# Keeping B's operands in DRAM, splitting two of seven products again, and weighing A's rows on ScalarE, in a 4096-cubed matmul with GELU

## The chip, the cores and the metric

The kernel runs on one core of a Trainium2 chip. Its time is the device time of the execution in microseconds (us). Before the change it took 1579.29 us (median of three runs). The traces are of single executions, so their spans differ by a few us from the medians.

Words used throughout: TensorE multiplies (PE in the profile; PEld is its weight load), VectorE (DVE) adds, subtracts and transposes, ScalarE (ACT) copies out of PSUM and applies functions, GpSimd (POOL) and SyncE (SP) issue DMAs. VectorE and ScalarE do their instructions in program order; the case in group 4 below shows VectorE idle for 8.13 us with a sum waiting behind a late transposition.

## The reference

```python
m, k, n = 4096, 4096, 4096            # a, b: random normal, float32
x = np.matmul(a, b)
return 0.5 * x * (1 + np.tanh(np.sqrt(2 / np.pi) * (x + 0.044715 * x**3)))
```

## The kernel before

It multiplies in fp16 by Strassen's scheme at the level of the whole matrices: each of A, B and the result has four quadrants, and seven products M1 to M7 replace eight. The result is made in 16 groups: a row block of A (four of them, 512 rows in each half) by a column block of B (four, 512 columns in each half). A group is 7 products of 64 matmuls, done in 4 steps each. A step is 16 matmuls of 128x512. Operand sums are made by VectorE two steps ahead, in three rotating buffers:

```python
PRODUCTS = [
    ("M3", "Y", "11", ("12", "22", 1)),          # name, chain, operand of A, operand of B
    ("M5", "X", ("11", "12", -1), "22"),
    ("M7", "X", ("12", "22", -1), ("21", "22", 1)),
    ...                                            # M1, M4, M2, M6
]
# in make_sums: one 128x2048 sum for one step
    t = pool.tile([P, 4 * NC], F16, name=tag, tag=tag, bufs=AHEAD + 1)
    nc.vector.tensor_tensor(out=x, in0=y, in1=z, op=ALU.add if o[2] > 0 else ALU.subtract)
```

A block of A comes in eight chunks of 1 MB in fp16 (quadrant and half of its depth), cast from float32 by four DMAs of 256 KB from GpSimd into one of two staging buffers, then turned by VectorE with one transposition of 2.3 us. The next block is loaded while the last group of the old one and the first group of the new one run (group gi and gi+1; `at(group, product, step, ...)`):

```python
            if na:                                 # the next group has another block of A
                at(gi, 4, c, load, (load_a, (mb1, "11", c)))
                at(gi, 5, 2 * c, turn_a, mb1, "11", c)
                at(gi, 5, 2 * c + 1, load, (load_a, (mb1, "12", c)))
                at(gi, 6, 2 * c, turn_a, mb1, "12", c)
                ...                                # "22" and "21" in the same manner
```

A step takes 3.45 us. B is read anew, cast by DMA, in nearly every group. A guard sums squares of A and B over rows and columns and falls back to a plain bf16 multiplication if magnitudes vary too much; ScalarE squares and VectorE adds, on the blocks in the form in which they are multiplied (A's turned). A's blocks change between groups 3 and 4, 7 and 8, 11 and 12.

## Time and profile before

| | before |
|---|---|
| median time | 1579.29 us |
| TensorE busy | 1567.7 us, 99% |
| VectorE, ScalarE busy | 1233.7 us (78%), 518.0 us (33%) |
| TensorE's waits | 4.2 us in four places |
| HBM traffic | 285 MB read, 67 MB written |
| a 256 KB piece of A, issue to landing (median) | 6.8 us |

The prediction below shows the lines behind the first rows and reads them. Two more lines are in the view of DMA issues (tile written and read, queue, operation, count, size, median us from issue to landing):

```profile
stage<-in_a_dram POOLq DMA_DIRECT2D x112, 256.0 KB, 6.8
```

and in the list of all waits (waiting engine, tile and line; what ended the wait; us in total, times, longest):

```profile
DVE aT L161 <- DMA stage<-in_a_dram: 39.9, 14, 10.8
```

VectorE's transposition waits for A's pieces now and then, most of it at the start, but TensorE never notices.

### The profile page before, as it was taken

How to read it: one execution, taken by the hardware profiler on the slowest of the kernel's cores; microseconds unless marked ns; L12 is line 12 of the kernel's file. 1: busy time of each engine (PE TensorE's matmuls, PEld its weight loads, DVE VectorE, ACT ScalarE, POOL GpSimd, SP SyncE). 2: the span in 40 equal slices, each digit the busy share in tenths (PEclk: the TensorE clock that was granted, in tenths of full speed). 3: DMA queues.
4: the chain of work that ended last, by engine and by line, in shares of the span. 5: the costliest groups of instructions: out<-in, count | busy, mean ns of one | idle time of the engine just before them, and what ended most of it. 6: DMA issues, size and time to landing. Idle time of an engine off the chain costs nothing. (4 is left out here: it accounts for less than half of the span.)

```text
span 1577.1 us, 19678 instructions
## 1 busy us (share of the span) xinstructions
PE 1567.7 (99%) x7246; PEld 709.6 (45%) x7246; DVE 1233.7 (78%) x1381; ACT 518.0 (33%) x710; POOL 537.7 (34%) x980
## 2 busy tenths in 40 slices
PE   9999999999999999999999999999999999999998
PEld 4444444444444444444444444444444444444443
DVE  1698888967787888895778778887687778988775
ACT  1036445311122545531111344542211145364111
POOL 7753442420234144341124413245011443314400
PEclk9999999999999999999999999999999999999999
DMA  9999884882968378686597937679468885747802
GB/s 173 198 215 189 132 162 79 161 162 48 193 106 158 87 131 160 108 179 115 87 161 117 186 72 142 146 113 182 79 121 146 134 160 93 151 105 134 161 28 82
DMA packets 225047, 211.13 MB, mean 134 GB/s; under 512 B 20144, under 2 KB 192176, under 8 KB 224944
## 3 DMA queue, kind: packets, MB, share of 16 engines
q0 software_dynamic: 187648, 142.67, 61.7%
q1 hardware_dynamic: 37296, 67.13, 11.8%
q8 instruction: 59, 0.97, 0.2%
q14 instruction: 44, 0.36, 0.1%
HBM read 285.22 MB, written 67.11 MB: 223 GB/s over the span
## 5 line engine op out<-in xcount | busy, mean ns | idle before, releaser
L331 PEld LDWEIGHTS <-aS 128*128 128x128 f16 x4960 | 485.3, 98 | 587.2 <-issue 2.2
L186 POOL DMA_DIRECT2D bR<-in_b_dram x832 | 447.6, 544 | 700.0 <-DVE bS L302 329.7
L302 DVE TENSOR_TENSOR aS<-aT 128x2048 f16<-128x2048 f16 (+1 forms) x312 | 376.1, 1212 | 151.0 <-PE accX L331 114.5
L331 PE MATMUL accX<-bS,aS 128*128 128x512 f16 x1984 | 431.1, 379 | 0.0
L302 DVE TENSOR_TENSOR bS<-bR 128x2048 f16<-128x2048 f16 x310 | 376.1, 1218 | 69.3 <-PE accX L331 58.5
L331 PEld LDWEIGHTS <-aT 128*128 128x128 f16 x1984 | 194.2, 98 | 234.8 <-issue 0.8
L422 ACT ACTIVATE y<-y 128x512 f32<-128x512 f32 x192 | 118.5, 630 | 351.8 <-DVE y L431 351.4
L331 PE MATMUL accY<-bS,aS 128*128 128x512 f16 x992 | 216.7, 379 | 1.8 <-DVE y L431 1.8
L331 PE MATMUL accY<-bS,aT 128*128 128x512 f16 x992 | 216.9, 379 | 0.5 <-DVE bS L302 0.5
L331 PE MATMUL accX<-bS,aT 128*128 128x512 f16 x992 | 216.7, 379 | 0.0
L331 PE MATMUL accX<-bR,aS 128*128 128x512 f16 x992 | 216.7, 379 | 0.0
L331 PE MATMUL accY<-bR,aS 128*128 128x512 f16 x992 | 216.7, 379 | 0.0
L186 POOL DMA_DIRECT2D stage<-in_a_dram x144 | 89.9, 630 | 249.0 <-DVE aT L161 178.0
L431 DVE TENSOR_TENSOR energy<-energy,square 128x1024 bf16<-128x1024 bf16 x240 | 164.4, 685 | 9.5 <-ACT square L207 5.7
L395 ACT COPY x<-accX 128x512 f32<-128x512 f32 x128 | 74.9, 585 | 224.3 <-PE accX L331 224.3
L207 ACT ACTIVATE square<-aT 128x1024 bf16<-128x1024 f16 x120 | 123.4, 1051 | 70.6 <-DVE energy L431 70.2
L207 ACT ACTIVATE square<-bR 128x1024 bf16<-128x1024 f16 x120 | 123.0, 1050 | 62.5 <-DVE energy L431 60.5
L161 DVE STREAM_TRANSPOSE aT<-stage 128x2048 uint32<-128x2048 uint32 (+1 forms) x37 | 74.6, 2017 | 46.0 <-DMA stage<-in_a_dram 39.9
L395 ACT COPY m<-accX 128x512 f32<-128x512 f32 x60 | 34.7, 579 | 215.7 <-PE accX L331 213.6
L422 ACT ACTIVATE y<-accX 128x512 f32<-128x512 f32 x64 | 38.2, 597 | 100.1 <-PE accX L331 99.9
L431 DVE TENSOR_TENSOR x<-accX,x 128x512 f32<-128x512 f32 x64 | 44.0, 691 | 21.8 <-ACT y L422 19.1
L431 DVE TENSOR_TENSOR y<-accY,m 128x512 f32<-128x512 f32 x60 | 39.9, 687 | 12.5 <-ACT m L395 12.4
(38 smaller groups left out, 344.9 us busy)
## 6 DMA issues: line engine op xcount, KB each, us to landing
bR<-in_b_dram POOLq DMA_DIRECT2D x832, 128.0 KB, 5.2
out_dram<-y SPq DMA_DIRECT2D x256, 256.0 KB, 5.7
stage<-in_a_dram POOLq DMA_DIRECT2D x112, 256.0 KB, 6.8
stage<-in_a_dram POOLq DMA_DIRECT2D x32, 128.0 KB, 5.1
row<-seen_d SPq DMA_DIRECT2D x2, 1.5 KB, 4.2
seen_d<-seen SPq DMA_DIRECT2D x1, 3.0 KB, 7.4
```

Source lines behind the costliest of these rows:

```text
L161: nc.vector.transpose(dst[:, :, x, :], src[:, :, x, :])
L186: nc.gpsimd.dma_start(out=dst, in_=src)
L207: nc.scalar.activation(t[:, :], src, ACT.Square)
L302: nc.vector.tensor_tensor(out=x, in0=y, in1=z, op=ALU.add if o[2] > 0 else ALU.subtract)
L331: nc.tensor.matmul(acc[:, :], sa[:, j // 2, i * P : (i + 1) * P, j % 2], sb[:, j, :], start=start and j == 0, stop=stop and j == 3, skip_g ...
L395: nc.scalar.copy(out=t[:, :], in_=src[:, :])
L422: nc.scalar.activation(y[:, :], src[:, :], ACT.Gelu_apprx_tanh)
L431: nc.vector.tensor_tensor(out=o[:, :], in0=x[:, :], in1=y[:, :], op=op)
```

## The change

Its intent is fewer matmul columns. In six groups M3 and M5 are each split by the same seven-product scheme again, one level down. That needs more and other sums, so to free VectorE the operands of B are made once, written to DRAM and fetched later; and the sums of squares of A leave VectorE for ScalarE, which squares each staged row with an accumulated output. The core of the diff (cuts marked):

```diff
+SPLIT_GROUPS = (8, 11, 12, 13, 14, 15)
+CHECK_GROUP = 9
+TURNS = ((2, 2), (3, 1), (5, 2), (6, 1), (7, 0), (7, 3), (8, 2), (9, 1))
+    def weigh_rows(mb, quad, c, xs):
+        s = staged[mb, quad, c]
+        ...
+            nc.scalar.activation(
+                weighed[mb, quad, c][:, :RUN], s[:, x, :], ACT.Square, accum_out=weighed[mb, ih][:, k, x : x + 1]
+            )
+            if tag == "bS" and gi == last_raw[nb]:
+                keep_operand((nb, name, q // 2), q % 2, t[:, :])      # SyncE writes it to DRAM
+    def multiply_split(gi, s, p):                                     # one of seven subproducts
+        for r in range(RT // 2):
+            ...
+            for j in range(NJ):
+                wide = p == "2" and j == 0
+                nc.tensor.matmul(banks[chain, i][:, :] if wide else out, ..., 256 columns if not wide)
+        ...                                                           # joins between regions of PSUM
-                at(gi, 4, c, load, (load_a, (mb1, "11", c)))
-                ...
+        for (quad, c), n in zip(chunks, turns):
+            do(n - 3, load, (load_a, (mb, quad, c)))
+            if turned:
+                do(n, turn_a, mb, quad, c)
+            for x in range(3):
+                do(n + x, weigh_rows, mb, quad, c, list(range(NX))[x * 6 : (x + 1) * 6])
+    stage_block(0, [first_step[CHECK_GROUP] + 3 + 4 * x for x in range(len(chunks))], turned=False)
+    def fetch(key, x):
+        t = split_tiles[key] = ring_tile(x, "bK")
+        nc.gpsimd.dma_start(out=t, in_=kept_unit(*key[1:])[:, :])
```

A's first block is reloaded from group 9 on only to be weighed. Every load of A now stands three steps ahead of its turn; in groups 8 and 12 the last three of the eight have steps of a split pair for this, half as long (the very last two such steps and a full one).

## The prediction

> **What bounds the kernel now.** I read the page's first two parts first: which engine is busy, and whether it is busy everywhere.
>
> ```profile
> PE 1567.7 (99%) x7246; PEld 709.6 (45%) x7246; DVE 1233.7 (78%) x1381; ACT 518.0 (33%) x710; POOL 537.7 (34%) x980
> PE   9999999999999999999999999999999999999998
> DVE  1698888967787888895778778887687778988775
> PEclk9999999999999999999999999999999999999999
> DMA  9999884882968378686597937679468885747802
> ```
>
> TensorE is busy in every slice at full clock; VectorE comes next. A busy TensorE can still be badly fed, since ends of matmuls are modelled, so I looked at what TensorE waited for (first fence: us in total, times, longest) and at how many matmuls start in equal stretches (second fence: busy us and count of each engine, then clock, DMA share, GB/s).
>
> ```profile
> PE accY L331 <- DVE y L431: 1.8, 1, 1.8
> PE accX L343 <- DVE table L583: 1.4, 1, 1.4
> PE accY L331 <- DVE bS L302: 0.5, 1, 0.5
> PE accY L362 <- DMA bR<-in_b_dram: 0.5, 1, 0.5
> ```
>
> ```profile
> 0.00:100.00 100.00, 98.09 (x440) 43.65 (x441) 52.19 (x57) 15.63 (x26) 72.31 (x132) 1.00 1.26 190
> ...
> 300.00:400.00 100.00, 100.00 (x465) 45.37 (x464) 75.26 (x81) 20.62 (x34) 27.45 (x48) 1.00 0.68 124
> 400.00:500.00 100.00, 100.00 (x465) 45.37 (x464) 78.36 (x74) 16.31 (x28) 32.76 (x59) 1.00 0.81 140
> ```
>
> All waits together are 4.2 us, and 465 matmuls start per 100 us almost everywhere: 215.05 ns for each 128x512 matmul, with no gaps. The chain of waits confirms little here: it lists only the last ACTIVATE. So the time is the number of moving columns, plus about 14 us before the first useful matmul and 5 us after the last. Only fewer columns, or new gaps, can move it. Work taken from VectorE, ScalarE or GpSimd gains nothing by itself.
>
> **What the Trainium skill says.** "TensorE: Matmul & The Clock Gate", section "Back-to-back issue gap", gives N/2.4 + 2.5 ns for a warm isolated matmul: 215.8 ns at 512 columns and 109.2 at 256. This trace has 215.05, so it agrees within 1 ns. The same section gives 131 ns per load-and-matmul pair at N=512; the trace contradicts that. Its ground for hope at 256 columns is 81 ns per pair at N=128: weight loads keep up. This trace has a weight load before every matmul, mean 98 ns, hidden under a 215 ns interval; no run here shows it under a 107 ns one.
>
> "ScalarE: Activation LUTs", section "What ACT_TABLE_LOAD costs", gives 186 ns + 0.833 ns per column for an ACTIVATE. The trace's 128x1024 squares take 1050 ns (the formula: 1039), so I use it for 256 columns: 399 ns.
>
> "DMA: Bandwidth & Descriptors", section "Issuing engines are not separate DMA queues", says that DMAs of all issuing engines share the same 16 DMA engines and interleave. So the kept copies compete with loads and results. The trace's own rates follow below.
>
> **The change, part by part.** I call one (row block, column block) pair of the outer order a group; there are 16. A full group is 7 products x 64 matmuls = 448, or 96.3 us.
>
> *Columns removed.* In groups 8, 11, 12, 13, 14 and 15, M3 and M5 each become seven subproducts of 16 matmuls with 256 columns; two of those 112 are 512 wide. Columns per product fall from 64x512 = 32768 to 110x256 + 2x512 = 29184, or 10.9%, while matmuls and weight loads rise from 64 to 112. The listing of the changed program has 576 more matmuls, which is 12 x 48. Time before: 64 x 215.05 ns = 13.76 us. After, the trace's overhead is 215.05 - 213.33 = 1.7 ns, the skill's 2.5, so I estimate 108.8 ns: 110 x 108.8 + 2 x 215 = 12.40 us. Saving 1.365 us per product, times 12 products: **16.4 us**. All of it lies on the bounding engine.
>
> *B's operands kept.* Groups 0 to 5 still read B; in groups 1, 2, 4 and 5 each column block's 14 MB of operands are written to DRAM and later groups fetch them. VectorE makes 160 fewer B sums (310 to 150 in the listing): 160 x 1.218 = 195 us. Off the path, so worth room, not time.
>
> *A's sums.* Each split group needs 14 sums for M3 and M5 instead of 4; 60 more x 1.219 = 73 us. The joins add 96 VectorE operations on 128x256 from PSUM; 128x512 takes 0.69 us, of which I take 0.15 as fixed, so 0.42 us each, 40 us.
>
> *Weighing A.* 120 of the 240 square-additions leave VectorE (120 x 0.685 = 82 us), with about 10 us of folding. ScalarE loses 128 squares of 1.05 us (134 us) and gets 512 of 399 ns (204 us); joins add 48 copies of 256 columns, some 0.37 us each or 18 us. Sums: VectorE 1234 - 195 + 73 + 40 - 92 = 1060 us; ScalarE 518 - 134 + 204 + 18 = 606 us. Neither becomes the bound on average.
>
> *Transfers.* From the page, the casting loads moved 142.67 MB in 61.7% of 16 engines' 1577 us, or 0.147 MB/us; results moved 67.13 MB in 11.8%, or 0.361 MB/us. Group 4 must now take 8.4 MB of B and about 3 MB of A as cast loads (78 us), plus 14.7 MB kept and 4.2 MB of results (52 us): 130 us of load in 96 us, a share of 1.35. Group 9, which reloads A's first block only to weigh it while it fetches 14.7 MB and writes 7.3 MB of split operands, comes to 1.27. The first 100 us ran at 1.26 with TensorE hardly waiting, so shares over 1 are possible (packets overlap); but these groups sit at the edge.
>
> *New gaps.* In a split pair TensorE needs VectorE's joins back within two short steps: 16 matmuls at 109 ns is 1.75 us, so 3.5 us. In groups 11, 13, 14 and 15 I count for the pair 14 sums (17.1), 16 joins (6.7) and 4 combinations (2.8), or 26.6 us against 24.8 us of TensorE, but about a third of the sums are made beforehand. In groups 8 and 12, behind a change of A's block, three transposes of 2.3 us join them. Following VectorE's order there by hand, the join in front of M3's seventh subproduct ends about 1 us late, and another 1 to 2 us later still if A's block lands late. I allow 2 us for groups 8 and 12 together, and 1 us for waits on transfers elsewhere: **+3 us**.
>
> Sum: 1579.3 - 16.4 + 3 = **1566 us**.
>
> **The rivals.**
>
> First, weight loads become the bound. A split subproduct needs one every 109 ns and their mean is 98 ns. For it: the margin is thin[...]. Against: 98 ns fits, and the loads show no effect at all on the 215 ns interval. At 125 ns per pair a product takes 110 x 125 + 430 = 14.2 us, longer than 13.76: 12 x 0.42 = 5 us lost, so about 1587 us.
>
> Second, transfers take over. Kept writes hold sum buffers (three in rotation, two steps ahead), and A's blocks get three steps from load to turn, only 5 us by step count inside a split pair, where the before kernel's loads of A took a median of 6.8 us to land and were given four or five steps. VectorE and ScalarE execute in order, so a late block holds everything behind it. Against: GpSimd may issue earlier than the step, and two steps of 3.44 us are a cushion. If groups 4, 8, 9 and 12 each lose 5 us, the gain vanishes: about 1583 us.
>
> Third, ScalarE's weighing in bursts of six (2.4 us) delays the copies out of PSUM: after M5, M7 and M1 each bank must be copied within three bank turns, 3 x 0.86 = 2.6 us, before TensorE accumulates on it again. The bursts are spread so that they end in time if A has landed; a cost of 0.5 us in each of about ten places gives 1571 us.
>
> A gain over 2% (31.6 us) has no source: even subproducts without overhead or gaps save 12 x (32768 - 29184)/2.4 ns = 17.9 us.
>
> **Range and chances.** The clean case is 1562 to 1563. Gaps only add, so the range is lopsided: 1561 to 1577. Slower by over 2% (above 1611) needs both rivals at more than twice their size: 3%. Faster by over 2%: 1%.
>
> **What would show it.** Right: 256-column matmuls at about 109 ns start to start, a split pair of about 24.8 us, TensorE's waits grown from 4 to under 10 us, VectorE near 1060 us and ScalarE near 606. Wrong: split stretches with fewer than about 900 starts per 100 us and no recorded wait (weight loads), or TensorE waiting on joins, sums or PSUM copies in groups 4, 8, 9 or 12, behind VectorE or ScalarE that itself waited for a transfer. A total under 1560 would mean that something outside the matmuls was on the path after all.

## More of the kernel before

In the program the loads of the eight chunks stand 4, 5, 3, 3, 4, 4, 8 and 11 steps ahead of their turns; GpSimd issues them earlier when its own order and the staging buffers allow it.

## The result

The changed kernel took 1661.52 us (median of 4 runs, 1657.83 to 1664.61) and is 5% slower: ratio 1.0517, 95% interval 1.0495 to 1.0539. A ratio here is the mean time of one kernel's fast runs over that of the other's fast runs of the same rounds, so not quite the ratio of the medians quoted.

The page of the changed kernel, first the busy time of each engine, then the span in 40 slices (tenths busy, granted TensorE clock, DMA share):

```profile
PE 1576.4 (95%) x7822; PEld 772.1 (46%) x7822; DVE 1067.3 (64%) x1241; ACT 658.4 (40%) x1654; POOL 370.2 (22%) x658
...
PE   9999999999799999999869997999897799999998
...
PEclk9999999999899999999989998999998899999999
DMA  9999999975989975998995899987979849385652
```

VectorE fell to 1067 us, as counted. TensorE now has holes, and its clock dips with them. The windows view (busy us and instruction counts of PE, PEld, DVE, ACT, POOL, then clock, DMA share, GB/s) shows where:

```profile
400.00:500.00 100.00, 84.03 (x368) 36.62 (x366) 71.84 (x75) 68.30 (x207) 25.34 (x45) 0.93 0.87 205
...
800.00:900.00 100.00, 79.00 (x435) 44.82 (x434) 57.05 (x62) 61.23 (x220) 19.83 (x33) 0.88 1.05 260
...
1200.00:1300.00 100.00, 85.71 (x487) 48.82 (x486) 62.54 (x70) 64.25 (x230) 23.77 (x39) 0.93 1.04 241
...
1400.00:1500.00 100.00, 100.00 (x576) 56.17 (x575) 62.38 (x78) 22.22 (x42) 9.68 (x18) 1.00 0.66 244
```

The worst stretches are those with much ScalarE work, which here means weighing A; but 1100:1200, not shown, also loses 7.6 us with ScalarE busy for only 24. So this is a hint and no proof. The last row is the change at its best: splits, fetches, no load of A, no hole.

To place the loss I took the start of each group's first matmul from the trace and subtracted the clean time of its matmuls. A clean group lasts 96.7 us, or 215.85 ns per matmul; the prediction's 215.05 came from counting starts in windows, where matmuls that overlap the edge are counted too. A clean split pair lasted 24.88 us. Here is the timeline of TensorE (start us, us, what) over one:

```profile
1152.96 3.87 PE L483 MATMUL accY<-bK,aS 128*128 128x512 f16 x32
1156.67 1.91 PE L483 MATMUL accY<-bK,aT 128*128 128x256 f16 x16
...
1174.35 3.66 PE L483 MATMUL accX<-bK,aS 128*128 128x256 f16 x32
1177.84 2.32 PE L401 MATMUL accX<-bK,aS 128*128 128x512 f16 x10
```

From 1152.96 to 1177.84 there are 224 matmuls, four of them 512 wide: (24.88 - 4 x 0.216)/220 = 109.2 ns per 256 columns. The rest is loss. Lost us by groups, in the profiled execution of each kernel (the experiments are explained below; the expectations count from 215.05 ns a matmul and so name some 5 us more in all):

| kernel | 0-2 | 3-4 | 5-6 | 7-8 | 9-10 | 11-12 | 13-15 | sum |
|---|---|---|---|---|---|---|---|---|
| before | 3.3 | 0 | 0 | 0 | 0 | 0 | 0 | 3.3 |
| changed | 3.5 | 22.7 | 0 | 29.9 | 14.7 | 34.7 | 0 | 105.5 |
| no weighing (e1) | 8.4 | 4.2 | 0 | 27.8 | 0 | 28.1 | 0 | 68.5 |
| weighed after the turn (e2) | 3.8 | 30.6 | 0 | 34.8 | 13.4 | 35.1 | 0 | 117.7 |
| no split (e3) | 6.8 | 22.6 | 0 | 10.6 | 0 | 5.2 | 0 | 45.2 |
| weighing alone (e4) | 3.5 | 15.6 | 0 | 0.2 | 17.3 | 0.6 | 0 | 37.2 |
| no accumulator reads (e5) | 5.1 | 13.2 | 0 | 25.2 | 14.6 | 30.0 | 0 | 88.1 |
| no weighing, early loads (e6) | 6.0 | 3.5 | 0 | 15.4 | 0 | 7.3 | 0 | 32.2 |
| no weighing, four splits (e7) | 4.2 | 3.8 | 0 | 12.4 | 0 | 2.8 | 0 | 23.2 |
| traffic alone, on before (e16) | 3.0 | 8.4 | 0 | 9.5 | 0 | 9.3 | 0 | 30.2 |

Check of the sums: 105.5 - 3.3 lost, less 6 x (27.63 - 24.88) = 16.5 saved, is 85.7 us; the spans of the two profiles differ by 1663.0 - 1577.1 = 85.9.

Beyond the 3.5 us at the start, which the kernel before has too, every us is lost where a block of A loads: at its three changes and, in group 9, at the reload. Groups that only keep, fetch, make split operands, or split (2, 5, 6, 10, 13 to 15) lose next to nothing. TensorE's waits now (against 4.2 us before):

```profile
PE accX L401 <- ACT x L513: 24.8, 6, 11.7
PE accY L483 <- DVE accY L498: 18.0, 2, 9.5
PE accX L401 <- ACT m L513: 13.2, 5, 4.1
PE accX L401 <- DVE aS L365: 8.3, 1, 8.3
PE accY L401 <- DVE y L549: 6.8, 2, 5.3
```

It waits for PSUM copies by ScalarE (x, m), joins of a split pair (L498) and sums of A (aS). None of these is slow in itself. What held the two engines stands in the list of all waits:

```profile
POOL stage L206 <- ACT scrap L228: 121.1, 11, 28.8
ACT scrap L228 <- DMA stage<-in_a_dram: 107.2, 15, 15.9
...
DVE aT L181 <- DMA stage<-in_a_dram: 87.7, 16, 10.7
```

ScalarE's weighing waited 107 us for pieces of A and VectorE's transpositions 88 (40 before). GpSimd for its part waited 121 us for the weighing to release a staging buffer before it could load. Pieces took a median of 11.1 us to land:

```profile
stage<-in_a_dram POOLq DMA_DIRECT2D x144, 256.0 KB, 11.1
```

The timelines of GpSimd, VectorE and TensorE show one case in group 4. In brackets is the idle time before and what ended it:

```profile
428.09 2.55 POOL L206 DMA_DIRECT2D stage<-in_a_dram  x4 [10.63 <-ACT scrap L228]
435.76 2.31 DVE L181 STREAM_TRANSPOSE aT<-stage 128x2048 uint32<-128x2048 uint32 x1 [8.13 <-DMA stage<-in_a_dram]
439.84 12.74 PE L401 MATMUL accX<-bR,aS 128*128 128x512 f16 x48 [8.32 <-DVE aS L365]
```

The load waits for ScalarE and goes out at 428; VectorE, idle, waits for it until 435.8; the sum that TensorE needs stands behind the transposition in VectorE's queue, and TensorE stops for 8.3 us.

A stop costs more than its length:

```profile
1011.98 16.82 PE L401 MATMUL accX<-bK,aT 128*128 128x512 f16 x64 [11.69 <-ACT x L513]
```

64 matmuls took 16.82 us after an 11.69 us wait, against 13.98 us elsewhere. "TensorE: Matmul & The Clock Gate" of the Trainium skill, Part 1, says that the clock falls to half after an idle window of about 3.4 us and needs about as long a busy one to come back. The trace agrees in kind: between the matmuls its clock record has 11 pieces at half clock, 79 us in all and each one to four times 3.4 us long (the kernel before has only one piece, of 5 us, after its last matmul). Each of the nine stops of 3.1 us and more has such a piece at it, a stop of 2.96 us has none, and two of 2.5 us have one. Counted from start to start, the matmuls in these pieces cost about 21 of the 105.5 us.

The longest stop, this one in group 9, can be followed back. ScalarE's order before it:

```profile
1008.25 0.42 ACT L228 ACTIVATE scrap<-stage 128x256 bf16<-128x256 f16 x1 [15.88 <-DMA stage<-in_a_dram]
...
1011.37 1.05 ACT L513 COPY x<-accX 128x512 f32<-128x512 f32 x2
```

ScalarE sat idle for 15.88 us in front of a row of a late piece, then weighed six rows in 3.1 us, and only then came the copy for which TensorE waited. Here it is the late data that cost most, not the length of the burst.

### The profile page after: what moved, and what is told of

Its sections match the earlier page's. It is cut to its first block, busy times and chain, and to the rows that moved or that the text cites. A ratio compares the mean times of both kernels' runs of the same rounds, so it can differ in the third digit from the quotient of the medians.

```text
span 1663.0 us, 21601 instructions
## 1 busy us (share of the span) xinstructions
PE 1576.4 (95%) x7822; PEld 772.1 (46%) x7822; DVE 1067.3 (64%) x1241; ACT 658.4 (40%) x1654; POOL 370.2 (22%) x658
## 5 line engine op out<-in xcount | busy, mean ns | idle before, releaser
L401 PE MATMUL accX<-bK,aS 128*128 128x512 f16 x1536 | 343.2, 386 | 24.0 <-ACT m L513 10.2
L763 DVE TENSOR_TENSOR aS<-aT 128x2048 f16<-128x2048 f16 x206 | 243.9, 1216 | 86.7 <-PE accX L401 62.1
L401 PE MATMUL accY<-bK,aS 128*128 128x512 f16 x1280 | 279.9, 381 | 5.3 <-DVE y L549 5.3
L228 ACT ACTIVATE scrap<-stage 128x256 bf16<-128x256 f16 x512 | 212.8, 416 | 121.6 <-DMA stage<-in_a_dram 107.2
L206 POOL DMA_DIRECT2D bR<-in_b_dram x320 | 173.0, 544 | 229.4 <-DMA bR<-in_b_dram 104.5
L401 PE MATMUL accX<-bS,aS 128*128 128x512 f16 x704 | 155.3, 382 | 7.0 <-ACT x L513 3.3
L365 DVE TENSOR_TENSOR aS<-aT 128x2048 f16<-128x2048 f16 (+1 forms) x112 | 133.9, 1200 | 35.6 <-PE accX L401 25.1
L401 PE MATMUL accX<-bK,aT 128*128 128x512 f16 x640 | 142.6, 384 | 11.7 <-ACT x L513 11.7
L365 DVE TENSOR_TENSOR bS<-bR 128x2048 f16<-128x2048 f16 x110 | 133.7, 1217 | 19.3 <-PE accX L401 14.5
L228 ACT ACTIVATION_READ_ACCUMULATOR scrap<-stage 128x1 f32 x512 | 95.5, 187 | 0.0
## 6 DMA issues: line engine op xcount, KB each, us to landing
bK<-k_M POOLq DMA_DIRECT2D x116, 1024.0 KB, 10.6
stage<-in_a_dram POOLq DMA_DIRECT2D x144, 256.0 KB, 11.1
k_M<-bR SPq DMA_DIRECT2D x16, 1024.0 KB, 12.4
```

The lines of the kernel that those rows point to most:

```text
L206: nc.gpsimd.dma_start(out=dst, in_=src)
L228: nc.scalar.activation(weighed[mb, quad, c][:, :RUN], s[:, x, :], ACT.Square, accum_out=weighed[mb, ih][:, k, x : x + 1])
L401: nc.tensor.matmul(acc[:, :], sa[:, j // 2, i * P : (i + 1) * P, j % 2], sb[:, j, :], start=start and j == 0, stop=stop and j == 3, skip_g ...
L763: nc.vector.tensor_tensor(out=t, in0=y, in1=z, op=ALU.add if op > 0 else ALU.subtract)
```

## The experiments

I numbered the runs e1 to e17. Beside the table above, each has its time against the kernel before in the same rounds. Where the guard's numbers for A are set to a constant, the product is still right and the guard merely does not look at A. All 17 results were correct.

### What the weighing costs: e1, e2, e4, e5, e15

**e1, no weighing.**

```diff
-            nc.scalar.activation(..., s[:, x, :], ACT.Square, accum_out=...)
-        nc.vector.tensor_reduce(out=stats["a"][...], in_=t...)
+        nc.vector.memset(stats["a"][...], 4096.0)
-    stage_block(0, [first_step[CHECK_GROUP] + ...], turned=False)
```

> The changed kernel without ScalarE's weighing of A's rows and without the reload of A's first block in group 9 (A's entries of the guard are set to a constant, so the guard no longer looks at A; the product is right). In the changed kernel 110 us of TensorE time are lost, all in groups 3-4 (23), 7-8 (31), 9 (15) and 11-12 (35), where blocks of A are loaded; groups 1, 2, 5, 6, 10 and 13-15 lose nothing. Theory S (the staging buffer, and with it the next load, is held by ScalarE's weighing): VectorE's turn alone now frees the buffer, loads start up to 10 us sooner, and the loss goes almost wholly: 1562 to 1572 us. Theory T (transfers: kept copies and fetches slow A's loads): loads stay slow at 9.6 us or more to landing, VectorE still waits for them, only group 9's 15 us and part of ScalarE's waits go: 1620 to 1645 us. Theory J (the split's joins stall groups 8 and 12): 1590 to 1620 us.

Measured: 1624.21 us (1619.93 to 1631.4), ratio 1.0287. The loss in groups 3-4 falls from 22.7 to 4.2 us and in group 9 from 14.7 to nothing. At the other two changes 28 us each remain. So weighing with its reload explains a little over a third of it, 37 of 102 us. (e1 drops the bytes of the reload too, so group 9's part is not ScalarE's alone.) The total lies in theory T's band. Theory S as a whole is wrong: TensorE still waits behind VectorE, and VectorE behind A's pieces, of which a median one takes 11.5 us to land.

**e2, the same squares, read from the turned block,** so that the turn alone frees the staging buffer.

```diff
-        s = staged[mb, quad, c]
+        src = staged[mb, quad, c] if mb == 0 else a_tiles[mb, quad, c].rearrange(...)
```

> The same 512 squares with accumulation on ScalarE at the same places, but those of blocks 1 to 3 read the turned block instead of the staging buffer, so that VectorE's turn alone frees the buffer (the guard's numbers for A then mean something else; the product is right). ScalarE's time stays near 658 us. Theory S: the loss in groups 3-4, 7-8 and 11-12 goes, group 9's reload (still weighed from staging) keeps its 15 us: 1575 to 1590 us. Theory W (ScalarE's bursts themselves, 3.24 us for six rows with the accumulator reads instead of my 2.4, delay the copies out of PSUM): nothing much changes, 1645 us or more. Theory T: above 1625 us.

Measured: 1674.27 us (1672.01 to 1676.48), ratio 1.0599, 13 us slower than the changed kernel. With the buffer free sooner the loss stays, although GpSimd's wait for that buffer is the longest of the waits around A's loads. In its place ScalarE waits 89 us for VectorE's turn, in order, before copies that TensorE needs. As e2 brings this new wait, it refutes theory S's numbers but does not show that holding the buffer costs nothing; the total fits theories W and T alike.

**e4, the weighing part of the change alone.** No split, nothing kept, B read in every group as before.

```diff
-SPLIT_GROUPS = (8, 11, 12, 13, 14, 15)
+SPLIT_GROUPS = ()
-    N_RAW = NNB + 2
+    N_RAW = len(groups)
-            if tag == "bS" and gi == last_raw[nb]:
+            if False:
-    ...                                            # also cut: the copies of B's blocks that are used as they are
```

> The weighing part alone: no group split, no operand kept, every block of B read and summed as in the kernel before; A's rows weighed by ScalarE from staging, at the changed places, group 9's reload included. Theory S: the loss at A's three changes appears without any kept operand, some 20 us each, and a smaller one in group 9: 1630 to 1660 us. Theory T: no kept copies or fetches, so almost no loss: 1578 to 1592 us. VectorE has all sums to make here, so a stall may cost more than in the changed kernel.

Measured: 1611.83 us (1609.78 to 1612.01), ratio 1.0204. Between the theories, and the table says why: 15.6 us in groups 3-4, where ScalarE also squares B (32 squares, as in the changed kernel), 17.3 at the reload, whose bytes lift the DMA share of group 9 to 1.14 here, and only 0.8 at the two other changes. This points to other work on ScalarE as what makes weighing costly at a change. The loads have their three steps of lead here too, but full steps, and a median piece lands in 6.8 us, as before the change: three full steps of lead do little harm at that landing time.

**e5, squares without the accumulated output.** ScalarE's two groups of the changed kernel (count | busy us, mean ns of one | idle before and what ended most of it):

```profile
L228 ACT ACTIVATE scrap<-stage 128x256 bf16<-128x256 f16 x512 | 212.8, 416 | 121.6 <-DMA stage<-in_a_dram 107.2
...
L228 ACT ACTIVATION_READ_ACCUMULATOR scrap<-stage 128x1 f32 x512 | 95.5, 187 | 0.0
```

The 416 ns are near the 399 that I had taken. The second line I had not expected: each row needs a further instruction of 187 ns to read the accumulator. Rows start 0.54 us apart, so six rows take 3.24 us of a step of 3.45.

```diff
-                ..., s[:, x, :], ACT.Square, accum_out=weighed[mb, ih][:, k, x : x + 1]
+                ..., s[:, x, :], ACT.Square
```

> The changed kernel with the 512 squares of A's rows kept at their places, reading the staging buffer, group 9's reload kept, but without the accumulated output, so without the 512 accumulator reads (187 ns each, 95.5 us; rows started 0.54 us apart with them). The guard's numbers for A are a constant; the product is right. Theory W (ScalarE is overfull where six rows a step, 3.24 us of 3.44, meet squares of B and copies out of PSUM): ScalarE falls to about 550 us, the loss in groups 3-4 falls from 23 to under 8 us and group 9's from 15 to under 5; groups 7-8 and 11-12 keep 28 each as without weighing, so 1625 to 1640 us. Theory S (the load waits for the weighing, whatever its length): groups 3-4 keep more than 15 us, 1645 us or more.

Measured: 1646.58 us (1645.49 to 1647.18), ratio 1.0428. 15 us come back: 9.5 in groups 3-4 (22.7 to 13.2) and 4.7 at each of the other changes; group 9 does not move. The total lies in theory S's band and groups 3-4 between the two. ScalarE fell to 612 us and not to 550, since the reads overlap the squares in part: rows start 0.45 us apart without them, 0.54 with them. Theory W has part of it, and my number for it missed.

**e15, four rows a step instead of six,** on top of e2.

```diff
-            for x in range(3):
-                do(n + x, weigh_rows, ..., list(range(NX))[x * 6 : (x + 1) * 6])
+            for x in range(4):
+                do(n + x, weigh_rows, ..., list(range(NX))[x * 4 : (x + 1) * 4])
```

> The run that weighs from the turned block (1674 us; 31 us lost in groups 3-4) with four rows in each of four steps instead of six, six and four in three; four rows take 2.2 us of a step. If the bursts' length is what holds the copies out of PSUM: groups 3-4 lose under 12 us, 1630 to 1655 us. If ScalarE's wait in order for late blocks is: 1665 us or more.

Measured: 1654.76 us (1651.22 to 1661.82), ratio 1.0485; 19.5 us better than e2 (medians), groups 3-4 from 30.6 to 19.5 us. The total is at the top of the band that I gave to burst length, the groups above it. So the length of the bursts is a part, ScalarE's wait in order for late data another. Group 9 reacted to neither shorter bursts nor missing accumulator reads, and its one long stop was followed back to late data above. How the 18.5 us that weighing costs in groups 3-4 divide stays open.

### What the split and the lead of the loads cost: e3, e6, e7

**e3, no split.**

```diff
-SPLIT_GROUPS = (8, 11, 12, 13, 14, 15)
+SPLIT_GROUPS = ()
-        made = gi == maker[nb]
+        made = False
```

> No group is split (no split operands made or kept either); kept operands, fetches and weighing stay. The clean split pairs in groups 11 and 13-15 took 24.9 us against 27.5, so six splits should be worth 16 us. Theory S or T: the loss at A's changes stays, perhaps smaller in groups 8 and 12 because a step is 3.44 us there instead of 1.75, so 1640 to 1675 us. Theory J: the loss in groups 8 and 12 goes (some 45 us), plus 16 us lost columns: 1625 to 1640 us.

Measured: 1618.26 us (1615.23 to 1623.3), ratio 1.0248. Below every theory: taking the split away, with its 16.5 us of saved columns, makes the kernel 43 us faster. The loss at the second and third change falls by 49 us (64.6 to 15.8) and group 9's vanishes, although the reload is still there. A median piece of A lands in 8.0 us and not 11.1: splitting also brings traffic, which this run removes with it: four makers each write 7 MB of split operands (group 9 is one), and a split group fetches 3 MB more.

**e6, loads as early as the buffer allows,** without weighing.

```diff
-        for (quad, c), n in zip(chunks, turns):
-            do(n - 3, load, (load_a, (mb, quad, c)))
+        for k, ((quad, c), n) in enumerate(zip(chunks, turns)):
+            do(max(n - 7, turns[k - 2] + 1 if k > 1 else 0), load, (load_a, (mb, quad, c)))
```

> The kernel without weighing (1624 us, 74 us lost, 28 in each of groups 7-8 and 11-12), with each load of A issued as soon as the staging buffer is free (a step after the turn of the block two before, at most seven steps ahead) instead of three steps ahead. Theory L (three steps are too short a lead for a block that needs 10 to 16 us, most of all three half-length steps inside a split pair, 5.2 us): the loss in groups 7-8 and 11-12 falls below 8 us each, 1572 to 1590 us. Theory T (transfers saturate there, whenever they are asked for): 1610 us or more.

Measured: 1589.42 us (1585.84 to 1595.93), ratio 1.007; 35 us better than e1. The total just lies in theory L's band, groups 7-8 do not. The place of A's loads is a cause by itself. It is more than a count of steps, as GpSimd's and VectorE's timelines in e1 show:

```profile
801.08 2.31 DVE L181 STREAM_TRANSPOSE aT<-stage 128x2048 uint32<-128x2048 uint32 x1
808.17 0.57 POOL L749 DMA_DIRECT2D bK<-k_split  x1 [9.89 <-PE accY L389]
...
819.33 2.70 POOL L206 DMA_DIRECT2D stage<-in_a_dram  x4
```

The turn at 801 freed the staging buffer, but the load into it went out at 819: in GpSimd's order it stood behind three fetches that waited for TensorE. e6 puts it in front of two of them, and it goes out 6 us after that turn began and not 18. Whether e1 with the fetches on SyncE would gain as much was not run. The pieces themselves land no sooner in e6, 11.4 us against 11.5. And 15.4 us stay in groups 7-8, where the waits of TensorE are new ones:

```profile
PE accX L389 <- DMA bK<-k_M: 11.9, 3, 5.4
```

It now waits for fetches of kept operands: the earlier loads seem to go at the fetches' expense.

**e7, groups 8 and 12 not split,** without weighing, loads three steps ahead.

```diff
-SPLIT_GROUPS = (8, 11, 12, 13, 14, 15)
+SPLIT_GROUPS = (11, 13, 14, 15)
```

> The kernel without weighing, with groups 8 and 12, those behind a change of A's block, not split: four splits, worth 10.6 us. Theory L: without half-length steps under A's loads the loss at the changes falls from 28 us each to some 5 us; 1579 - 11 + 10 to 20 = 1577 to 1590 us. Theory T: fetches are 3 MB fewer in each of these two groups, so some relief too, but groups 7 and 11 keep their 4 to 8 us: 1585 to 1600 us.

Measured: 1590.34 us (1586.42 to 1593.37), ratio 1.0079; 34 us better than e1. The two splits behind a change of A's block save 5.5 us and cost 40 there (28 us lost at either change become 12.4 and 2.8). The total misses theory L's band by 0.3 us and lies in theory T's too: the edit takes away the half-length steps and 6 MB of fetches at once, and no run parts the two.

### What the traffic costs: e16, e9

**e16, traffic alone, added to the kernel before:** in the six groups where A's blocks load, B's operands are also written to DRAM. Nothing reads them.

```diff
+    LOADED = (3, 4, 7, 8, 11, 12)
+            if tag == "bS" and gi in LOADED:
+                nc.sync.dma_start(out=kept_unit(...)..., in_=t[:, :])
+    for gi in LOADED: ...                          # the 4 MB of B used as they are
```

> The kernel before with one thing added: in groups 3, 4, 7, 8, 11 and 12, where A's blocks load, the 14 MB of B operands of each group are also written to DRAM from where they lie, as the changed kernel does in groups 1, 2, 4 and 5 (nothing reads them). DMA share there rises from 0.7-0.8 to about 1.1, as high as in the changed kernel's groups 7-8. If traffic alone makes A's blocks late: A's pieces take 9 us or more instead of 6.8 and each of the three changes loses 8 to 25 us, 1600 to 1650 us. If the kernel before's four to five steps of lead and its weighing swallow it: under 4 us a change, 1578 to 1590 us.

Measured: 1613.71 us (1604.58 to 1618.31), ratio 1.0227. The total and the landing time are as expected of traffic. The kernel before, with no product split again and with its own weighing and leads, loses 27 us in the profiled run, the fastest of the four (34 us by the medians), when 14 MB of writes are added per group. The windows of groups 3 and 4 and the issue line of A:

```profile
314.00:411.00 97.00, 96.09 (x445) 43.41 (x444) 65.89 (x65) 16.40 (x28) 19.13 (x32) 1.00 0.99 261
411.00:508.00 97.00, 92.15 (x417) 41.32 (x417) 72.74 (x69) 16.33 (x28) 30.19 (x54) 0.96 1.11 270
```

```profile
stage<-in_a_dram POOLq DMA_DIRECT2D x112, 256.0 KB, 13.1
```

At a DMA share of 1.0 to 1.1 a piece of A takes 13.1 us instead of 6.8. VectorE's waits for A double, from 40 to 77 us, and sums wait 21 us for buffers that are still being written out. Those held buffers could be a rival cause, but the timelines of VectorE and TensorE show the late piece of A in front of the sum:

```profile
809.01 2.31 DVE L161 STREAM_TRANSPOSE aT<-stage 128x2048 uint32<-128x2048 uint32 x1 [8.24 <-DMA stage<-in_a_dram]
811.25 2.32 DVE L317 TENSOR_TENSOR bS<-bR 128x2048 f16<-128x2048 f16 x2
812.48 3.15 PE L351 MATMUL accY<-bS,aT 128*128 128x512 f16 x7 [6.86 <-DVE bS L317]
```

The same stands at the other two changes, stops of 5.55 and 6.97 us. This is the cleanest proof that traffic alone stops TensorE. It also corrects how I read the share: 1.26 in the first 100 us does not mean that there is room above 1 where a load is due. The changed kernel's groups 1 and 2, where no block of A loads, ran at 1.11 and 1.06 and lost 1.9 us and nothing.

**e9, fetches issued by SyncE instead of GpSimd.**

```diff
-        nc.gpsimd.dma_start(out=t, in_=kept_unit(*key[1:])[:, :])
+        nc.sync.dma_start(out=t, in_=kept_unit(*key[1:])[:, :])
```

> The changed kernel (1661 us) with only the 158 fetches of kept operands issued by SyncE instead of GpSimd; their bytes and places in the order are the same. In the trace of the run with early loads, GpSimd issued A's pieces and the fetches one by one, each waiting for a DMA some eight places back. Theory Q (one issuing queue: A's slow casting loads and the fetches hold each other up): A's pieces land in about 8 us instead of 11.1, the loss in groups 7-8, 9 and 11-12 falls by a third to a half, group 4's 21 us stay (no fetches there); 1610 to 1640 us. Theory T (the bytes themselves are too many at once, whoever issues them): 1650 us or more.

Measured: 1664.55 us (1662.95 to 1667.45), ratio 1.0539. No gain: with the weighing in place the issuer makes no difference, and the total lies in theory T's band. It agrees with the section of the skill's DMA page that the prediction named. A's loads, now free of the fetches, waited for ScalarE to release staging buffers (693 us in all), so e9 does not test their place behind fetches by itself.

### Putting it together: e8, e10 to e14, e17

**e8, a full kernel, guard whole:** six splits; early loads as in e6; A's later blocks weighed as in the kernel before, in groups 6, 9 and 14; only block 0 reloaded and weighed by rows, in groups 10 and 13.

```diff
-    stage_block(0, [first_step[CHECK_GROUP] + 3 + 4 * x for x in range(len(chunks))], turned=False)
+    turns = [first_step[10] + 4 + 6 * x for x in range(4)] + [first_step[13] + len(PAIR) + 1 + 5 * x for x in range(4)]
+    stage_block(0, turns, turned=False)
+    for gi in (6, 9, 14): ...                     # square, add_squares, weigh on the turned block
```

> A full kernel with the guard whole: six splits and kept operands as changed; A's loads early as in the run without weighing; blocks 1 to 3 of A weighed from the turned block by ScalarE and VectorE as in the kernel before (groups 6, 9 and 14, where VectorE has room), and only the first block reloaded and weighed by rows, four chunks each in groups 10 and 13, six or five steps apart. If lead and weighing are the causes: 1565 to 1585 us, at or just below the kernel before. If transfers are: 1600 us or more.

Measured: 1599.8 us (1598.11 to 1611.9), ratio 1.0152. Outside the band for lead and weighing and 0.2 us short of that for transfers; 42 us lost, 17.6 of it in groups 7-8. TensorE waited 13 us for fetches in all.

**e10, e8 with fetches by SyncE**, and **e11, the same with groups 8 and 12 not split** (edits as in e9 and e7).

> The repaired kernel (1600 us, 48 lost, 11 of them waiting for fetches in group 8) with the fetches issued by SyncE. Theory Q: no more waits of TensorE for fetches, group 8 loses under 6 us; total 1568 to 1582 us, within 1% of the kernel before. Theory T: 1590 us or more.

Measured: 1622.68 us (1619.47 to 1627.12), ratio 1.0279. Worse than e8 by 23 us: TensorE waited 28 us behind VectorE for sums of A. A single piece of A took up to 30.6 us to land, against 22.6 in e8. So here, unlike in e9, the issuer mattered; why was not followed up.

> The same with groups 8 and 12 not split: 5.3 us more of columns, but no half-length steps under A's loads and 6 MB fewer fetched in these two groups. If the splits behind a change of A's block still cost more than the 2.65 us that each saves: faster than the run with six splits, 1568 to 1578 us. If the loads now hide: 3 to 6 us slower than it.

Measured: 1606.16 us (1602.41 to 1607.65), ratio 1.017. e10's total lies in theory T's band, e11's in neither of its own, but the comparison holds: without the two splits the kernel is 16.5 us faster.

**e12, four splits, fetches by GpSimd again,** the split operands for group 13 made in group 8 instead of 7, squares of A's last block in group 12, block 0 reloaded in groups 13 and 14.

```diff
-SPLIT_GROUPS = (8, 11, 12, 13, 14, 15)
+SPLIT_GROUPS = (11, 13, 14, 15)
+    maker[groups[8][1]] = 8
-    for gi in (6, 9, 14):
+    for gi in (6, 9, 12):
+    turns = [first_step[gi] + len(PAIR) + 5 * x for gi in (13, 14) for x in range(4)]
```

> A full kernel with the guard whole, put together from what the runs showed: four splits (11, 13, 14, 15), so no half-length steps while A's blocks load into groups 8 and 12; the split operands of group 13's column block made in group 8 instead of 7; GpSimd issues the fetches again (SyncE was 23 us worse with six splits); A's loads as early as the buffer allows; blocks 1 to 3 weighed as in the kernel before in groups 6, 9 and 12; block 0 reloaded and weighed by rows, a chunk every five steps, in groups 13 and 14 where no other block of A moves. Columns save 10.6 us. If lead, half-length steps and weighing are what cost: under 20 us lost against 9 in the kernel before, 1572 to 1584 us. If traffic alone keeps A late: 1590 us or more.

Measured: 1582.14 us (1578.6 to 1584.83), ratio 1.001 (0.9987 to 1.0033). Within the band for lead, half-length steps and weighing. Groups 7-8 lose nothing, for the first time in a kernel that keeps operands; 9.1 us are lost in group 12. A's pieces still take 11.5 us to land, so the repair hides this and does not shorten it.

**e13, those last squares begun later** and folded at the start of group 13, and **e14, e13 with six splits** (and the operands for group 13 made in group 7 again, as group 8 then needs them).

```diff
+            if gi == 12:
+                n = position[gi, 2, 1] + x * 19 // 32
```

> The last kernel (1582 us; 9.4 us lost in group 12, 5.5 of them TensorE behind VectorE's additions of squares) with the squares of A's last block begun nine steps later in group 12, after all of that block has been turned, and folded at the start of group 13. If those additions waited for the squares of unturned data and held VectorE's queue: group 12 loses under 3 us, 1572 to 1577 us, 0.2 to 0.4% faster than the kernel before. If not: 1582 us again.

Measured: 1579.55 us (1575.96 to 1591.22), ratio 1.0018 (0.9993 to 1.0042): the same as the kernel before. Group 12 loses nothing, as expected, but group 13 now loses 3.7 us, and the total misses its band.

> The same with groups 8 and 12 split as well (and group 13's split operands made in group 7, as group 8 needs them). Saves 5.3 us of columns. If the splits behind a change of A's block lose more than they save (6 MB more to fetch, half-length steps under A's loads): groups 7-8 and 12 lose 10 to 25 us together and the total is 1580 to 1595 us. If early loads are all it needs: 1568 to 1572 us.

Measured: 1599.43 us (1591.0 to 1607.95), ratio 1.0118; 24.5 us lost in groups 7-8 and 7.1 in 11-12, more than either band allowed. Even with the weighing out of the way and early loads, the two splits behind a change of A's block, with the making moved to group 7, lose 20 us net of what they save.

**e17, e13 with the fold of those squares moved behind group 13's split pair.**

```diff
-        before.setdefault(first_step[gi + 1] + 2 if gi == 12 else ..., []).append((weigh, ("a",)))
+        before.setdefault(position[gi + 1, 2, 2] if gi == 12 else ..., []).append((weigh, ("a",)))
```

> The kernel with four splits (1579.6 us) with the fold of A's last squares moved out of group 13's split pair to after it. If the fold held the joins there: group 13 loses under 1 us instead of 4, 1574 to 1578 us; at this size the spread of runs (1576 to 1591 us) may hide it.

Measured: 1576.17 us (1572.92 to 1584.54), ratio 0.9984 (0.9953 to 1.0015). The loss in group 13 is gone, but group 12 lost 8.5 us in this profiled execution and nothing in e13's, so the runs differ by as much as the gain. This is the best median of all, not a proven improvement: the interval includes 1.

## Why the prediction was wrong

The prediction, 1566 us in 1561 to 1577, missed by 95 us.

- **Columns removed: right.** 109.2 ns per 256-column matmul against 108.8 estimated; a pair saves 27.63 - 24.88 = 2.75 us against 2 x 1.365 = 2.73, so six save 16.5 us against 16.4. The rival that weight loads become the bound is refuted by the clean pair.
- **VectorE: right**, 1067 us against 1060. **ScalarE: too low**, 658 against 606; the term that was missing is the accumulator read, 95.5 us, of which some 47 us do not overlap the squares (e5 without it: 612).
- **Transfers: the estimate of load was used wrongly.** I found shares of 1.27 to 1.35 for groups 9 and 4 and let them pass because the first 100 us had run at 1.26. Measured were 1.09 and 0.91, over groups that the stops had made longer. e16 shows that at 1.0 to 1.1 pieces of A take 13.1 us where they took 6.8.
- **The lead: read wrongly.** The prediction gives the loads of the kernel before "four or five steps"; its code has 3 to 11, and the chunk that was late in e16 is one of the two with three.
- **New gaps, "+3 us": the step that failed.** It measured 105.5 - 3.3 = 102 us: 22.6 in group 8 and 25.6 in group 12, for which 2 us were allowed, and the rest elsewhere, for which it was 1 us. I had followed joins by hand with data on time. The runs show in its place three causes at A's changes and the reload: the weighing (37 us by e1, of which the accumulator reads are some 15 by e5), A's loads standing three steps ahead and behind fetches in GpSimd's order (35 us by e6), and traffic (27 us alone by e16). They are not a sum, since each makes the others worse: removing the splits alone brought back 60 lost us (e3), because they bring both half-length steps and bytes.
- **The rivals.** The second named the mechanism, A's blocks late and engines in order behind them, with the right places (4, 8, 9 and 12), but allowed 5 us a group where 15 to 35 us a change were lost. The third, ScalarE's bursts, was allowed 0.5 us in ten places; e5 and e15 show 10 to 20 us. What no rival had was the clock: stops of some 3 us and more also slowed the matmuls after them, about 21 us.
- The sign that I named for a wrong prediction, waits in groups 4, 8, 9 and 12 behind engines that wait for a transfer, is what the trace showed.

What stays open: how ScalarE's share in groups 3-4 divides between bursts and waits in order; how the cost of the splits divides between half-length steps and bytes; why SyncE's fetches cost 23 us in e10 and nothing in e9; and why e17 loses 8.5 us in group 12 in one execution while e13 loses none.

## What to carry to other kernels

Where TensorE is fully fed, a change that removes columns must pay with nothing else on time-critical paths: ask of each load how long it takes to land under the traffic that the change adds, not under that of the kernel before, and compare it with the lead that the change leaves. Put waits for such loads only on engines that have no urgent work behind them in order. And count a stop of TensorE of some 3 us and more at more than its length: here stops of 82 us in all cost another 21 us at half clock.

## What the Trainium skill lacked or had wrong

- "ScalarE: Activation LUTs": it says that an ACTIVATE can give an accumulator output, not that reading it is an instruction of its own. Here 187 ns for each of 512, and rows of 256 columns start 0.54 us apart (0.45 us in e5, without the output), where its formula gives 0.4 us for one ACTIVATE.
- "TensorE: Matmul & The Clock Gate", section "Back-to-back issue gap": the isolated formula, 215.8 and 109.2 ns at 512 and 256 columns, fits streams with a weight load before every matmul, too (215.85 and 109.2 ns here); the 131 ns per load-and-matmul pair that the page gives for 512 columns does not.
- "DMA: Bandwidth & Descriptors", section "Anatomy of one DMA": 2.0 us plus bytes/436e3 gives 4.4 us for 1 MB (an estimate from its formula). Fetches of 1 MB took medians of 6.8 and 10.6 us in the changed kernel. The page gives no rule for how landing times grow under load; here a casting piece of 256 KB went from 6.8 us at a share of about 0.7 to 13.1 at 1.0 to 1.1.
